# Four products for the decay sums of the delta rule, and one weight split moved ahead of a tile's split at the start of the FFN

## The chip, the core and the metric

The kernel runs on one core of a Trainium2 chip. A core has five engines that run side by side and wait for each other by semaphores: TensorE (PE in the profile; its weight loads stand apart as PEld), VectorE (DVE), ScalarE (ACT), GpSimd (POOL) and SyncE (SP, which here only issues DMAs). Each engine works through its own list of instructions strictly in the order in which they were written into it. The metric is the device time of one execution in microseconds (us), and of several executions the median.

## The reference, cut to what matters

One decoder layer is computed for a prompt (512 tokens with 16 learned tokens ahead of them) and for 8 samples of 8 tokens. Two places of it matter here. In the delta rule the log decays `g` of each token and head are summed up inside their chunk:

```
gcum = jnp.cumsum(gc, axis=-1)
...
g_last = g_i[..., -1:]
s = (s * jnp.exp(g_last)[..., None]
     + jnp.einsum('bhcd,bhce->bhde', k_i * jnp.exp(g_last - g_i)[..., None], v_new))
```

so both the running sum and the sum over the whole chunk are needed. In the FFN the normalised input is multiplied by a matrix of 1024 rows and 2 x 2816 columns:

```
xn = rmsnorm(x, p['ln_ffn_pre'])
up, gate = jnp.split(xn @ p['w_ffn_in'], 2, axis=-1)
gate, new_ffn_conv = causal_dwconv(gate, ffn_conv_buf, p['ffn_conv_w'], p['ffn_conv_b'])
x = x + rmsnorm((jax.nn.gelu(gate) * up) @ p['w_down'], p['ln_ffn_post'])
```

## The kernel before

**Split products.** Large products are made of three fast ones: each operand is split into a rounded high part and the rest. `split` (lines 312 to 314) does that with a CAST on ScalarE (line 313) and a subtraction on VectorE (line 314); a product then takes high by high, low by high and high by low. All matmuls stand under line 271 of `mm`, all transposes under line 419, so the profile tells them apart by the names of their tiles.

**Decay sums.** `gdn_decays` (from line 588) has the tokens in five chunks: four of 128 tokens and a tail of 80 (`NTL`). For each chunk it multiplies a constant matrix (an upper triangle for the running sum, ones for the whole sum; others for the tail, which holds the samples and the learned tokens) by the chunk's `g` of 4 heads: 10 plain fp32 products of 4 columns each, into one PSUM tile that VectorE copies to `gc` (lines 605 and 606). TensorE meets them at 71.5 us, among the projections and the attention over the cache.

**Start of the FFN.** The end of `out_proj` interleaves the output projection's last products with the first products of the FFN. The normalised rows come in five tiles of tokens (`TILES`); `turn(i, end)` transposes one tile on TensorE into two PSUM tiles, and `put_f` splits these into the blocks that the FFN multiplies by: `fhi`/`flo` with a tag of two figures, the first for the upper or lower half of the 1024 rows, the second for the half of the tokens. The fifth tile (`turn(4, ...)`) goes into `fhi12`/`flo12` and `fhi22`/`flo22`, the second half of the tokens. `turn` also returns `sums`, three VectorE operations that start the sums for the later steps.

**First steps.** The FFN's 22 blocks of 128 columns are run one after the other. The first three (`PLAIN`) are done plainly, by `plain_g` (gate) and `plain_u` (up), each for two halves of the tokens; the rest by a seven-product scheme with sums of weights (`sw`, split into `hw`/`lw`) and of inputs (`gf`, `fhit`, `flot`). `ffn_in` takes over from `out_proj` with the first half of step 0 done, then issues the first half of step 1 (`plain_g(sts[1], 0)`, whose weights were split in `out_proj`, and `plain_u(sts[1], 0)`, whose weights `plain_w(0, 1)` loads as two `wraw` tiles and splits into `hw`/`lw`), then the second halves of step 0 and step 1, then step 2.

**What sets the order.** The program is written as Python calls in one order; a scheduler then lays out each engine's list with a model of its own, moving instructions where data allow. Pools hold a fixed number of buffers per tag (3 `wraw`, 2 `whi`, 6 `hw`), so a load waits until the tile three loads back has been split. SP issues the loads of weights in order, each wait holding up all that come after.

Of the kernel before, what the change touches and what calls it, by code (L numbers as in the profile page):

```python
# [33 lines left out]
NS = NB * TS  # L34
# [8 lines left out]
CHUNKS = tuple((128 * c, 128) for c in range(4)) + ((CS, NS + NM),)  # L43
TAIL = 4
NTL = NS + NM
# [105 lines left out]
class Body:  # L151
# [437 lines left out]
    def gdn_decays(self):  # L589

        nc = self.nc
        nch = len(CHUNKS)

        def kept(tag):
            return self.t(self.keep, [128, nch, H], tag)

        p = self.ps("t")[:, : 8 * nch].rearrange("p (c e) -> p c e", e=8)
        for i, (c0, n) in enumerate(CHUNKS):
            up = self.c("upper_t", n) if i == TAIL else self.c("upper")
            tot = self.c("same_t", n) if i == TAIL else self.c("ones")  # L600
            self.mm(p[:n, i, 0:4], up, self.g[:n, i, :], start=True, stop=True)
            self.mm(p[:n, i, 4:8], tot, self.g[:n, i, :], start=True, stop=True)
        self.gc = self.t(self.keep, [128, nch, 8], "gc")
        nc.vector.memset(self.gc, 0.0)
        nc.vector.tensor_copy(self.gc[:, 0:4], p[:, 0:4])
        nc.vector.tensor_copy(self.gc[:NTL, 4], p[:NTL, 4])
        self.neg_eg = kept("neg_eg")
        nc.scalar.activation(self.neg_eg, self.gc[:, :, 0:4], AF.Exp)
        nc.vector.tensor_scalar(self.neg_eg, self.neg_eg, -1.0, None, op0=ALU.mult)
        self.ek = kept("ek")  # L610
        nc.vector.tensor_tensor(out=self.ek, in0=self.gc[:, :, 4:8], in1=self.gc[:, :, 0:4], op=ALU.subtract)
        nc.scalar.activation(self.ek, self.ek, AF.Exp)
# [971 lines left out]
    def out_proj(self, pool, wo0, swo, sm):  # L1584
# [9 lines left out]
        ys, sums, ends = {}, {}, {}  # L1594
# [41 lines left out]
        def turn(i, end):  # L1636
            n, xs, ps = self.TILES[i][1], ys.pop(i), []
            with self.tc.issue_after(end):
                for g in range(2):
                    p = self.ps4("t")  # L1640
                    for k in range(4):
                        ch = 4 * g + k
                        self.transpose(p[:, k, :n], xs[:n, 128 * ch : 128 * ch + 128])
                    ps.append(p)
            c = 128 * ((i - 1) % 2) + 34
            c = slice(c, c + 128)
            for g, p in enumerate(ps):
                if i:
                    self.put_f(g, i > 2, c, p)
                else:  # L1650
                    self.put_f(g, 0, slice(32, 34), p[:, :, NS : NS + 2])
                    for half in range(2):
                        self.put_f(g, half, slice(0, 32), p[:, :, 32 * half : 32 * half + 32])

            def sums():
                r1, r2 = (r[:, :, c] for r in self.r12)
                h11, l11 = (e.bitcast(F32)[:, :, c] for e in f["11"])
                nc.vector.tensor_tensor(out=r1, in0=ps[0], in1=h11, op=ALU.subtract)
                nc.vector.tensor_tensor(out=r1, in0=r1, in1=l11, op=ALU.subtract)
                nc.vector.tensor_tensor(out=r2, in0=ps[1], in1=r1, op=ALU.subtract)  # L1660

            return sums

        def first(c0):
            w, ps = self.weight(a["w_ffn_in"][0], c0), self.psd()[:, :NC]
# [3 lines left out]
        n = self.TILES[0][1]  # L1669
# [8 lines left out]
        product(2, 1)  # L1678
        finish(2)
        turn(0, ends[2, 1])  # L1680
        product(3, 0)
        turn(1, ends[3, 0])
        product(4, 0)
        swo.close()
        self.ftpool = self.pool(sm, "ft", side="right")
        turn_consts = self.ffn_consts()
        self.r12 = [self.t(self.ftpool, [128, 4, NC], tag) for tag in ("fhit4", "flot4")]
        turn(2, ends[4, 0])
        product(3, 1)
        finish(3)  # L1690
# [5 lines left out]
        w1 = [self.t(self.ftpool, [128, 8, 128], tag, F32R) for tag in ("fhit3", "flot3")]  # L1696
# [94 lines left out]
    def ffn_in(self, firsts, sf, gx):  # L1791
# [76 lines left out]
        def begin(st):  # L1868
            st["pre"] = self.t(pool, [128, 514 + 80], "fpre", bufs=2)
# [85 lines left out]
        def plain_w(c0, m):  # L1955
            if m == 1 and c0:
                return w1
            if m != 1:
                return self.weight(w, c0 + 128 * m)
            his, los = [], []  # L1960
            for raw in self.raw_w(w, c0 + 128 * m):
                hi, lo = (self.t(w7, [128, 4, 128], tag, F32R, bufs=n) for tag, n in (("hw", 6), ("lw", 6)))
                self.split(hi, lo, raw)
                his += [hi[:, k] for k in range(4)]
                los += [lo[:, k] for k in range(4)]
            return his, los
# [16 lines left out]

        def plain_u(st, half):
            if not half:
                st["wu"] = plain_w(0, st["m"])
            ps = self.psd()[:, :NC]
            end = self.plain(ps, st["wu"], half)
            st["u", half] = ps
            return end  # L1990
# [4 lines left out]

        sts, waiting = [{"m": m} for m in range(PLAIN)], []
        st = sts[0]
        (st["wg"], ps, _), (st["wu"], u, _), w1, more = firsts
        begin(st)
        copy_g(st, 0, ps)  # L2000
        st["u", 0] = u
        plain_g(sts[1], 0)
        end = plain_u(sts[1], 0)
        more()
        sums = self.sums(gx)
        next(sums)
        with self.tc.issue_after(end):
            plain_g(st, 1)
            conv(st)
            plain_u(st, 1)  # L2010
        plain_end(st)
        next(sums)
        st = sts[1]
        with self.tc.issue_after(end):
            plain_g(st, 1)
            conv(st)
            plain_u(st, 1)
# [16 lines left out]
        for m in range(PLAIN, NF):  # L2034
            st = nxt
# [194 lines left out]
```

## Time and profile before

| | |
|---|---|
| time, median of 3 executions | 1150.32 us |
| the three | 1149.95, 1150.32, 1154.78 us |
| time of the profiled execution | 1154.05 us |
| its span in the profile | 1152.3 us |
| mean granted TensorE clock in it | 0.993 |
| PE busy | 1123.5 us, 98% |
| DVE busy | 715.7 us, 62% |
| ACT busy | 539.0 us, 47% |
| POOL busy | 220.6 us, 19% |
| DMA, mean | 136 GB/s |

The profile is of one execution: all times in it count from the span's start. A row of the timeline has the start, the duration, the engine, the line, the operation, its tiles (out<-in), their shape, and in brackets the idle time of the engine ahead of it with what ended it. Matmuls overlap, so the distance from start to start, not the duration, is what one costs in a row of many. "PEclk" is the TensorE clock that the throttle granted, as a share of full speed.

### The profile page before, as it was taken

Reading aid. Unit: us, or ns where it says so; the run is one execution under the profiler, and the core shown is the slowest. Engines: PE = TensorE matmul, PEld = TensorE weight load, DVE = VectorE, ACT = ScalarE, POOL = GpSimd, SP = SyncE. Lnnn points to the kernel's source line nnn. Section 1 sums busy time; section 2 is a strip of 40 time slices with the busy share of each in tenths; the row PEclk is TensorE's granted clock in tenths of the full one; section 3 lists DMA queues with packets and bytes.
Section 4 is the critical chain, followed back from the end, with each engine's and each line's share of the span. In section 5 each row is a group of like instructions: output and inputs, shape, how many; then the busy total and the mean of one; then the engine's idle time right before and its main releaser. Section 6 shows DMA issues by size and latency. Waiting matters only on the chain.

```text
span 1152.3 us, 23630 instructions
## 1 busy us (share of the span) xinstructions
PE 1123.5 (98%) x8689; PEld 1009.0 (88%) x8689; DVE 715.7 (62%) x1874; ACT 539.0 (47%) x1308; POOL 220.6 (19%) x344
## 2 busy tenths in 40 slices
PE   8999999999999999999999999999999999999997
PEld 7987887787787787789999977899999999999996
DVE  5456666695485386484343764499889898832323
ACT  5234545464465365442432444365555655732321
POOL 3122221120120010010000003323445444200000
PEclk9999999999999999999999999999999999999998
DMA  6366336737746856822232454223333332432322
GB/s 190 81 222 191 107 98 200 250 109 261 246 145 220 292 176 209 262 64 74 56 94 65 128 175 147 91 73 102 102 87 100 93 94 73 144 96 75 102 75 82
DMA packets 184205, 157.04 MB, mean 136 GB/s; under 512 B 12555, under 2 KB 146258, under 8 KB 184089
## 3 DMA queue, kind: packets, MB, share of 16 engines
q1 hardware_dynamic: 179569, 147.01, 42.0%
q0 software_dynamic: 3264, 5.16, 1.5%
q10 hardware_dynamic: 1256, 3.35, 1.0%
q8 instruction: 69, 1.13, 0.4%
q14 instruction: 47, 0.39, 0.1%
HBM read 145.60 MB, written 9.88 MB: 135 GB/s over the span
## 4 chain that ended last, share of the span: by engine, by line
PE 77%; issue 13%; ACT 3%; DVE 3%; POOL 3%; DMA 1%; DVEq 0%; POOLq 0%; ACTq 0%; SPq 0%
PE ps_d L271 28%; PE ps_t L271 18%; PE ps_g L271 15%; PE ps_s L271 7%; PE ps_t L419 7%; ACT KT L1420 1%; PE ps_m L271 1%; POOL grr L383 1%; POOL gf L383 0%; DVE cy L671 0%; DMA page<-in_cache_v 0%; POOL hss L383 0%; PE lnb L271 0%; ACT whi L313 0%; ACT st L877 0%
## 5 line engine op out<-in xcount | busy, mean ns | idle before, releaser
L271 PE MATMUL ps_d<-xhi,whi 128*128 128x256 f32 (+2 forms) x704 | 218.7, 311 | 0.4 <-ACT xhi L313 0.4
L314 DVE TENSOR_TENSOR wlo<-wraw,whi 128x512 fp32r<-128x512 f32 (+1 forms) x194 | 135.8, 716 | 126.0 <-ACT whi L313 125.3
L271 PE MATMUL ps_d<-xhi,wlo 128*128 128x256 f32 (+2 forms) x704 | 214.1, 304 | 0.0
L271 PE MATMUL ps_d<-xlo,whi 128*128 128x256 f32 (+2 forms) x704 | 213.9, 304 | 0.1
L313 ACT CAST whi<-wraw 128x512 fp32r<-128x512 f32 (+1 forms) x198 | 117.4, 612 | 180.0 <-PE ps_d L271 97.0
L271 PEld LDWEIGHTS ps_d<-xhi,whi 128*128 128x128 f32 x704 | 134.5, 191 | 6.1 <-issue 3.8
L271 PEld LDWEIGHTS ps_d<-xlo,whi 128*128 128x128 f32 x704 | 134.8, 192 | 3.1 <-issue 2.4
L271 PEld LDWEIGHTS ps_d<-xhi,wlo 128*128 128x128 f32 x704 | 134.7, 191 | 1.6 <-issue 1.0
L1420 ACT COPY KT<-ps_t 128x512 f32<-128x512 f32 x106 | 57.2, 603 | 31.3 <-PE ps_t L419 30.8
L419 PE MATMUL ps_t<-consts,page 128*128 128x128 f32 x512 | 67.8, 279 | 0.3
L271 PE MATMUL ps_t<-fhit,hw 128*128 128x290 f32 x228 | 68.0, 298 | 0.0
L271 PE MATMUL ps_t<-flot,hw 128*128 128x290 f32 x228 | 67.7, 297 | 0.0
L271 PE MATMUL ps_t<-fhit,lw 128*128 128x290 f32 x228 | 67.6, 297 | 0.0
L419 PEld LDWEIGHTS ps_t<-consts,page 128*128 128x128 f32 x512 | 55.6, 140 | 13.7 <-issue 6.7
L313 ACT CAST hw<-sw 128x512 fp32r<-128x512 f32 x76 | 47.2, 622 | 41.3 <-PE ps_g L271 19.9
L314 DVE TENSOR_TENSOR lw<-sw,hw 128x512 fp32r<-128x512 f32 x76 | 59.7, 786 | 6.6 <-ACT hw L313 6.5
L271 PEld LDWEIGHTS ps_t<-flot,hw 128*128 128x128 f32 x228 | 43.3, 190 | 0.0
L271 PEld LDWEIGHTS ps_t<-fhit,lw 128*128 128x128 f32 x228 | 43.1, 189 | 0.0
L271 PEld LDWEIGHTS ps_t<-fhit,hw 128*128 128x128 f32 x228 | 43.0, 189 | 0.0
L1908 DVE SCALAR_TENSOR_TENSOR fy<-fpre,fw,fy 128x592 f32<-128x592 f32 x44 | 36.5, 830 | 2.2 <-ACT fy L1906 1.6
L271 PE MATMUL ps_s<-page,pT 128*32 128x256 f32 x512 | 35.1, 385 | 1.4 <-DMA page<-in_cache_v 1.3
L271 PE MATMUL ps_s<-KT,qb 128*32 128x256 f32 x512 | 35.7, 385 | 0.6
(693 smaller groups left out, 3000.6 us busy)
## 6 DMA issues: line engine op xcount, KB each, us to landing
page<-in_cache_k SPq DMA_DIRECT2D x128, 256.0 KB, 4.4
page<-in_cache_v SPq DMA_DIRECT2D x128, 256.0 KB, 4.2
wraw<-in_w_in SPq DMA_DIRECT2D x88, 256.0 KB, 3.1
wraw<-in_w_ffn_in SPq DMA_DIRECT2D x50, 256.0 KB, 3.1
wraw<-in_w_down SPq DMA_DIRECT2D x40, 256.0 KB, 3.2
raw<-in_w_ffn_in SPq DMA_DIRECT2D x38, 256.0 KB, 2.9
wraw<-in_w_out SPq DMA_DIRECT2D x16, 256.0 KB, 2.9
x<-in_x_prompt SPq DMA_DIRECT2D x4, 512.0 KB, 6.8
```

The lines of the kernel that those rows point to most:

```text
L271: return self.nc.tensor.matmul(out, lhsT, rhs, **kw).ins
L313: self.nc.scalar.copy(hi, raw)
L314: (eng or self.nc.vector).tensor_tensor(out=lo, in0=raw, in1=hi.bitcast(F32), op=ALU.subtract)
L383: nc.gpsimd.tensor_tensor(out=dst, in0=dst, in1=self.mhalf[:rows, :n], op=ALU.pow)
L419: self.nc.tensor.transpose(out, in_, self.ident[:k, :k])
L1420: copy(kt[:, :, 128 * j : 128 * j + 128], tp)
L1908: nc.vector.scalar_tensor_tensor(out=y, in0=pre[:, j : j + 592], scalar=fw[:, m, 16 + j : 17 + j], in1=y, op0=ALU.mult, op1=ALU.add)
```

## The change

Two edits. The decay sums are made in 4 products in place of 10: the four whole chunks lie beside each other in `g`, so one product of 4 x 4 columns takes all of them for the running sum and one for the whole sum, and the tail has its own two of 4 columns. And the up weights of step 1 are loaded and split by a call that stands ahead of the split of the fifth turned tile: `turn` no longer calls `put_f` for that tile itself but hands out `put`, which `ffn_in` calls after `plain_w(0, 1)`.

```
-        for i, (c0, n) in enumerate(CHUNKS):
-            up = self.c("upper_t", n) if i == TAIL else self.c("upper")
-            tot = self.c("same_t", n) if i == TAIL else self.c("ones")
-            self.mm(p[:n, i, 0:4], up, self.g[:n, i, :], start=True, stop=True)
-            self.mm(p[:n, i, 4:8], tot, self.g[:n, i, :], start=True, stop=True)
+        for e, (whole, tail) in enumerate((("upper", "upper_t"), ("ones", "same_t"))):
+            sl = slice(4 * e, 4 * e + 4)
+            self.mm(p[:, 0:4, sl], self.c(whole), self.g[:, 0:4, :], start=True, stop=True)
+            self.mm(p[:NTL, 4, sl], self.c(tail, NTL), self.g[:NTL, 4, :], start=True, stop=True)
...
-            for g, p in enumerate(ps):
-                if i:
-                    self.put_f(g, i > 2, c, p)
...
+            def put():
+                for g, p in enumerate(ps):
+                    if i:
+                        self.put_f(g, i > 2, c, p)
...
+            if i < 4:
+                put()
...
-            return sums
+            return sums if i < 4 else (put, sums)
...
         def plain_u(st, half):
             if not half:
-                st["wu"] = plain_w(0, st["m"])
+                st["wu"] = st.get("wu") or plain_w(0, st["m"])
...
-        (st["wg"], ps, _), (st["wu"], u, _), w1, more = firsts
+        (st["wg"], ps, _), (st["wu"], u, _), w1, (put, more) = firsts
+        sts[1]["wu"] = plain_w(0, 1)
+        put()
         begin(st)
```

On TensorE the rest of the list stays as it was; only the decay sums differ. Before, at the place of the decay sums (`xhi`, `xlo`, `whi` belong to a projection around them, `kvt` to new keys and values):

```order
L419 MATMUL ps_t_938<-consts_66,kvt_848 80x128
L271 MATMUL ps_d_980<-xhi_6_84,whi_972 128x256
L271 MATMUL ps_t_947<-g_661,consts_66 128x4 x8
L271 MATMUL ps_t_947<-g_661,consts_66 80x4 x2
L271 MATMUL ps_d_980<-xlo_7_85,whi_972 128x256
```

and now:

```order
L271 MATMUL ps_d_974<-xhi_6_84,whi_966 128x256
L271 MATMUL ps_t_947<-g_661,consts_66 128x4x4
L271 MATMUL ps_t_947<-g_661,consts_66 80x4
L271 MATMUL ps_t_947<-g_661,consts_66 128x4x4
L271 MATMUL ps_t_947<-g_661,consts_66 80x4
L271 MATMUL ps_d_974<-xlo_7_85,whi_966 128x256
```

Eight products of whole chunks became two, and the two of the tail stayed; their neighbours are the same.

ScalarE's list at the start of the FFN, before (`fhi12`, `fhi22` are the fifth tile, `fpre` the copied gate products of steps 0 and 1, `hw` the up weights of step 1):

```order
L313 CAST fhi12_1736_9258<-ps_t_1832_9880 128x4x128
L313 CAST fhi22_1740_9262<-ps_t_1833_9885 128x4x128
L1971 COPY fpre_1852_9922<-ps_d_1818_9768 128x258
L1972 COPY fpre_1852_9922<-ps_d_1818_9768 128x4x8
L1971 COPY fpre_1853_9925<-ps_g_1854_9926 128x258
L1972 COPY fpre_1853_9925<-ps_g_1854_9926 128x4x8
L313 CAST hw_1857_9957<-wraw_1855_9953 128x512
L313 CAST hw_1859_9961<-wraw_1856_9955 128x512
```

and now:

```order
L313 CAST fhi12_1736_9252<-ps_t_1832_9874 128x4x128
L313 CAST hw_1854_9916<-wraw_1852_9912 128x512
L313 CAST hw_1856_9920<-wraw_1853_9914 128x512
L313 CAST fhi22_1740_9256<-ps_t_1833_9879 128x4x128
L1975 COPY fpre_1858_9928<-ps_d_1818_9762 128x258
L1976 COPY fpre_1858_9928<-ps_d_1818_9762 128x4x8
L1975 COPY fpre_1859_9931<-ps_g_1860_9932 128x258
L1976 COPY fpre_1859_9931<-ps_g_1860_9932 128x4x8
```

The two weight casts moved past the second cast of the fifth tile and the four copies, but still stand behind the first cast of that tile. VectorE's list at the same place, before:

```order
L1660 TENSOR_TENSOR flot4_1798_9650<-ps_t_1820_9798,fhit4_1797_9649 128x4x128
L314 TENSOR_TENSOR flo12_1737_9259<-ps_t_1832_9880,fhi12_1736_9258 128x4x128
L314 TENSOR_TENSOR flo22_1741_9263<-ps_t_1833_9885,fhi22_1740_9262 128x4x128
L1658 TENSOR_TENSOR fhit4_1797_9649<-ps_t_1832_9880,fhi11_1734_9256 128x4x128
L314 TENSOR_TENSOR lw_1858_9958<-wraw_1855_9953,hw_1857_9957 128x512
L314 TENSOR_TENSOR lw_1860_9962<-wraw_1856_9955,hw_1859_9961 128x512
```

and now:

```order
L1664 TENSOR_TENSOR flot4_1798_9644<-ps_t_1820_9792,fhit4_1797_9643 128x4x128
L314 TENSOR_TENSOR flo12_1737_9253<-ps_t_1832_9874,fhi12_1736_9252 128x4x128
L314 TENSOR_TENSOR lw_1855_9917<-wraw_1852_9912,hw_1854_9916 128x512
L314 TENSOR_TENSOR lw_1857_9921<-wraw_1853_9914,hw_1856_9920 128x512
L314 TENSOR_TENSOR flo22_1741_9257<-ps_t_1833_9879,fhi22_1740_9256 128x4x128
L1662 TENSOR_TENSOR fhit4_1797_9643<-ps_t_1832_9874,fhi11_1734_9250 128x4x128
```

The two subtractions of the weights moved past two operations. Further down, some two dozen rows on VectorE and a dozen on ScalarE stand a few places earlier or later up to the middle of the first step of the seven-product scheme, and on SP two loads for that scheme (`raw`) now stand behind two loads of `wraw`; from there on all lists are as before.

More of the change, by code (lines that the diff above doesn't have):

```diff
@@ L1646, in turn @@
             c = slice(c, c + 128)
-            for g, p in enumerate(ps):
-                if i:
-                    self.put_f(g, i > 2, c, p)
[L1650 to L1653, printed above, removed]
+            def put():
+                for g, p in enumerate(ps):
+                    if i:
+                        self.put_f(g, i > 2, c, p)
+                    else:
+                        self.put_f(g, 0, slice(32, 34), p[:, :, NS : NS + 2])
+                        for half in range(2):
+                            self.put_f(g, half, slice(0, 32), p[:, :, 32 * half : 32 * half + 32])
+            if i < 4:
+                put()
             def sums():
```

## The prediction

> **What bounds the kernel now.** I read the page first, then the waits of TensorE by stretch, then the timeline at the two places of the change, then the granted clock in stretches of 3.41 us.
>
> ```profile
> PE 1123.5 (98%) x8689; PEld 1009.0 (88%) x8689; DVE 715.7 (62%) x1874; ACT 539.0 (47%) x1308; POOL 220.6 (19%) x344
> PE 77%; issue 13%; ACT 3%; DVE 3%; POOL 3%; DMA 1%; DVEq 0%; POOLq 0%; ACTq 0%; SPq 0%
> ```
>
> TensorE is busy 98% of the span and carries 77% of the chain that ended last. So a microsecond taken out of its list, or out of one of its waits, should reach the end unless a later wait swallows it. The waits of TensorE between the two places (74 to 748 us) and behind the second (754 to the end) are few:
>
> ```profile
> PE ps_s L271 <- DMA page<-in_cache_v: 1.3, 2, 0.9
> ...
> PE ps_t L419 <- ACT yT L2126: 0.8, 1, 0.8
> ```
>
> (us in total, times, longest; the first row is of 15 between the places, none over 2.0 us in total, the last is the longer of two behind.) Only the 1.3 us are on a DMA, and the loads of those pages are themselves let go by TensorE:
>
> ```profile
> SPq L1399 <- PE ps_t L419: 59.3, 35, 11.3
> SPq L1399 <- PE ps_s L271: 58.0, 28, 9.3
> ```
>
> So an earlier TensorE brings earlier loads, and I let all of an early gain through; the bound below is that none of it comes through.
>
> The clock is the less visible part. These are stretches of 3.41 us (PE busy with its instructions in brackets, then the granted clock):
>
> ```profile
> 71.03:74.44 3.41, 3.40 (x32) 1.00 1.04 364
> 74.44:77.85 3.41, 3.41 (x19) 0.50 1.05 383
> 712.73:716.15 3.42, 1.58 (x10) 1.00 0.38 153
> 716.15:719.56 3.41, 3.41 (x10) 0.50 0.46 159
> 746.87:750.28 3.41, 1.49 (x13) 1.00 0.83 236
> 750.28:753.69 3.41, 3.41 (x13) 0.50 0.45 130
> ```
>
> Three times behind the start the clock is halved for just one such stretch. The starts lie 641.71 and 34.13 us apart, 188 and 10 times 3.413: the stretches sit on a fixed grid, and each halved one follows one in which TensorE did little. In two of these it was idle about half the time; in the first it was "busy", but with 20 passes of four columns. Both places of the change stand there.
>
> **The change part by part: the decay sums.**
>
> ```profile
> 70.68 0.71 PE L419 MATMUL ps_t<-consts,kvt 128*128 128x128 f32 x5
> 71.52 2.23 PE L271 MATMUL ps_t<-g,consts 128*128 128x4 f32 x20
> 73.61 0.36 PE L271 MATMUL ps_d<-xlo,whi 128*128 128x256 f32 x1
> 72.65 1.10 PE L271 MATMUL ps_t<-g,consts 128*128 128x4 f32 x10
> ```
>
> Each fp32 product is two passes: 20 for 10 products, from 71.52 to 73.61, 2.09 us. The last row is of a view that starts later: the last ten passes (six of a whole chunk, four of the tail) take 73.61 - 72.65 = 0.96, so the ten whole ones ahead take 1.13, or 0.113 each. Twelve whole passes go: **1.36 us**. The four whole passes that stay have 16 columns, not 4. If they cost as much as passes of 128 columns, which run at (70.68 - 68.75) / 16 = 0.121 in this row,
>
> ```profile
> 68.75 2.10 PE L419 MATMUL ps_t<-consts,page 128*128 128x128 f32 x16
> ```
>
> 0.03 comes off; below, if nothing reaches the end, 0. I take 1.36, as TensorE is neither waiting just ahead of the next matmul nor just behind. `gc` is ready earlier and no one waits for it there.
>
> **The wait at the start of the FFN.** First columns are start and duration:
>
> ```profile
> 747.59 1.30 ACT L313 CAST fhi<-ps_t 128x512 fp32r<-128x512 f32 x2 [1.39 <-PE ps_t L419]
> 749.47 1.18 ACT L313 CAST hw<-wraw 128x512 fp32r<-128x512 f32 x2
> 748.21 1.40 DVE L314 TENSOR_TENSOR flo<-ps_t,fhi 128x512 fp32r<-128x512 f32 x2 [0.26 <-ACT fhi L313]
> 750.16 1.29 DVE L314 TENSOR_TENSOR lw<-wraw,hw 128x512 fp32r<-128x512 f32 x2
> 747.67 0.60 PE L419 MATMUL ps_t<-consts,y 128*128 128x128 f32 x4
> 750.18 0.55 PE L271 MATMUL ps_s<-fhi,hw 128*128 128x290 f32 x1 [1.92 <-ACT hw L313]
> 750.91 0.61 PE L271 MATMUL ps_s<-fhi,lw 128*128 128x290 f32 x1
> 732.46 1.04 SPq L309 DMA_DIRECT2D wraw<-in_w_ffn_in  x2
> ```
>
> TensorE waits 1.92 us for the first cast of the weights, and its third matmul for the first `lw`. The weights were asked for at 732.46 and so are long there; the casts only stood behind six others. In the new list the first weight cast still stands behind `fhi12`, which waits for the transposes: it starts one cast after 747.59, at 747.59 + 0.60 = 748.2 and ends near 748.8, so the first matmul starts at about 748.9. On VectorE `flo12` runs from 748.21 for 0.7 and the first `lw` from about 748.85 to 749.5: the third matmul starts at 749.57, not 750.91. Gain **1.34 us**. Between zero and 1.92 (no wait left) lie the bounds; since everything from the third matmul on hangs on that `lw`, I keep 1.34.
>
> What is late in its place: `fhi22`/`flo22` end 1.3 us later, near 750.85. They are first read in the second half of the next product, which starts at
>
> ```profile
> 755.19 0.30 PE L271 MATMUL ps_t<-fhi,whi 128*128 128x290 f32 x1
> 768.37 0.30 PE L271 MATMUL ps_g<-fhi,wlo 128*128 128x290 f32 x1
> 765.18 1.89 DVE L314 TENSOR_TENSOR wlo<-wraw,whi 128x512 fp32r<-128x512 f32 x3
> 773.72 1.75 POOL L1826 TENSOR_TENSOR sw<-raw,raw 128x512 f32<-128x512 f32 x1 [1.23 <-DVE lw L314]
> ```
>
> at 755.19 + 12 x 0.134 = 756.8, after the change 754.0 at the earliest: 3.1 us of cover. The four `fpre` copies move back 1 us and free PSUM that is wanted at 761.6. Two `raw` loads now stand behind a `wraw` load that waits for the new `lw`, some 4 us later than now; their first reader is GpSimd at 773.72. All these cost nothing while that cover lasts, and a microsecond of TensorE for each beyond it.
>
> **The clock.** What a halved stretch costs comes from the distances of starts, first at the decay sums, then at the FFN:
>
> ```profile
> 74.05 0.28 PE L271 MATMUL ps_d<-xlo,whi 128*128 128x256 f32 x1
> 74.17 0.28 PE L271 MATMUL ps_d<-xhi,wlo 128*128 128x256 f32 x1
> 74.79 0.41 PE L271 MATMUL ps_d<-xhi,whi 128*128 128x256 f32 x1
> 75.00 0.41 PE L271 MATMUL ps_d<-xlo,whi 128*128 128x256 f32 x1
> ...
> 752.05 0.44 PE L271 MATMUL ps_s<-fhi,hw 128*128 128x290 f32 x1
> 752.29 0.44 PE L271 MATMUL ps_s<-flo,hw 128*128 128x290 f32 x1
> 753.86 0.29 PE L271 MATMUL ps_s<-fhi,lw 128*128 128x290 f32 x1
> 753.99 0.30 PE L271 MATMUL ps_s<-fhi,hw 128*128 128x290 f32 x1
> ```
>
> 0.12 becomes 0.21, 0.13 becomes 0.24: of 3.41 us some 45% is lost, **1.53 us** each. After the change the low work of the decay sums lasts 0.73 us, not 2.09, and the FFN's wait is split into about 0.6 and 0.4 with matmuls between: neither leaves a stretch as empty as the 1.49 or 1.58 of 3.41 above, so I expect neither to halve the clock. The stretch behind 712.73 is not touched. Bounds for this term in one execution: 0 and 3.06.
>
> [...]
>
> **The sum.** Against the profiled execution: 1154.05 - 1.36 - 1.34 - 3.06 = 1148.3, and 1151.35 if the clock term is nothing. The median is another matter. It lies 3.73 us under the profiled execution, 2.4 times the price of a halved stretch; the grid starts anew against each execution, so I read the spread of the three times (1149.95 to 1154.78) as none to three such stretches. An execution like the median then had about 0.6 of them (3 - 2.4), two thirds of it at the two places: 0.4 x 1.53 = 0.6. So 1150.32 - 2.70 - 0.6 = 1147.0; I say **1147.1**.
>
> **The rivals.** A: *the wait moves on*. TensorE comes up to 2.9 us earlier to `ps_g` of step 2, whose third matmul (768.37) needs a `wlo` that ends near 765.9 now, 2.5 us ahead. In the new list that `wlo` stands behind the same operations as before, in another order, and VectorE has no gap in the 4 us ahead of it, so it can hardly come earlier. By the row lengths I get it some 0.9 to 1.3 us ahead of its matmul; if it is wrong by that much more, the wait gain goes: 1150.32 - 1.36 = 1149.0. [...] C: *the median holds all of both places' cost*: 1150.32 - 2.70 - 3.06 = 1144.6; against it stands the spread, in which the fastest lies only 0.4 below the median. D: *slower*. VectorE works strictly in order, and the convolution of step 0 (`fy`, line 1908) moved ahead of an operation that waits for nothing. `fy` waits for ScalarE, which waits for TensorE:
>
> ```profile
> 760.80 0.83 DVE L1908 SCALAR_TENSOR_TENSOR fy<-fpre,fw,fy 128x592 f32<-128x592 f32 x1 [1.36 <-ACT fy L1906]
> ```
>
> now 1.36 us idle. If that idle time grows, everything behind it, the `wlo` too, slips. It decides from the point at which `wlo` ends beyond 767.0 (768.37 - 1.34), and is slower than before once TensorE waits over 2.7 us, or 1.2 with a halved stretch behind it (1.53). Three microseconds of slip would give 1147.1 + 3 + 1.53 = 1151.6. Against it: `fy`'s input comes earlier too, by the same 1.34.
>
> **How the numbers follow.** Forecast 0.62 (1145.5 to 1148.9), A 0.12, B 0.09, C 0.13, D 0.04. The range goes from just above C's 1144.6 to A with one more halved stretch on a bad grid, 1149.0 + 1.5: 1144.9 to 1150.3. A measurement of this kernel tells about 0.5% (5.75 us) from no change, so faster begins at 1144.57 and slower at 1156.07. Half and more of C and a little of the forecast's edge lie beyond the first: 0.13. Of D only a slip of some 8 us would pass the second: 0.03. The rest, 0.84, is within 0.5%: a gain of 2 to 4 us that this bound does not tell from none.
>
> **What would show it.** Right: eight passes for `g` in about 0.75 us; the first `ps_s` matmul of step 1 some 0.6 us behind the transposes, no halved stretch behind either place, no wait of TensorE at `ps_g` of step 2. Wrong: a new TensorE wait on `wlo` or `flo`, the pitch of the four new passes far over 0.12, a halved clock behind one of the two places, or a median that moves by under 1 us.

## The result and the profile after

| | before | changed |
|---|---|---|
| median of the first comparison, 10 executions each | 1153.88 us | 1147.30 us (1145.09 to 1151.86) |
| median of a later one, 34 and 12 executions | 1152.31 us | 1148.25 us |
| span of the profiled execution | 1152.3 us | 1145.7 us |

The changed kernel takes 0.9957 of the time before (95% interval 0.994 to 0.9975), and 0.9973 (0.9958 to 0.9988) the second time: 3 to 7 us less by the first, 1 to 5 by the second. One execution of the later comparison on each side, 1348.90 us before and 3498.77 us changed, lies far from all others and is left out of its ratio. The rows of the changed kernel's page that answer to the first two of the prediction:

```profile
PE 1118.0 (98%) x8677; PEld 1003.2 (88%) x8677; DVE 727.3 (63%) x1874; ACT 532.2 (46%) x1308; POOL 229.0 (20%) x344
PE 76%; issue 12%; DVE 5%; ACT 3%; POOL 3%; DMA 1%; DVEq 0%; POOLq 0%; ACTq 0%; SPq 0%
```

Twelve TensorE instructions are gone, and the bound is the same. One row goes the wrong way: VectorE is 11.6 us longer busy with as many instructions; its `wlo` subtractions alone last 763 ns in the mean, not 716. This comes with the weight split (727.4 us and 757 ns with the split alone, 715.1 us and 715 ns with the sums alone), and no wait of TensorE shows for it. One place where an operation of VectorE lasts longer than elsewhere (`lw`, 1.62 us where it took 0.68) matters below.

The timeline of TensorE at the decay sums (start, duration):

```profile
70.30 0.90 PE L271 MATMUL ps_t<-g,consts 128*128 128x16 f32 x8
71.06 0.37 PE L271 MATMUL ps_d<-xlo,whi 128*128 128x256 f32 x1
```

From the first pass to the next product 0.76 us, where it was 2.09. At the start of the FFN, TensorE, ScalarE, VectorE and GpSimd:

```profile
743.49 0.60 PE L419 MATMUL ps_t<-consts,y 128*128 128x128 f32 x4
744.58 0.40 PE L271 MATMUL ps_s<-fhi,hw 128*128 128x290 f32 x1 [0.49 <-ACT hw L313]
745.39 0.40 PE L271 MATMUL ps_s<-fhi,lw 128*128 128x290 f32 x1 [0.28 <-DVE lw L314]
...
743.42 0.59 ACT L313 CAST fhi<-ps_t 128x512 fp32r<-128x512 f32 x1 [1.40 <-PE ps_t L419]
743.90 1.14 ACT L313 CAST hw<-wraw 128x512 fp32r<-128x512 f32 x2
...
744.65 2.38 DVE L314 TENSOR_TENSOR lw<-wraw,hw 128x512 fp32r<-128x512 f32 x2
...
744.87 1.60 POOL L1830 TENSOR_TENSOR sw<-raw,raw 128x512 f32<-128x512 f32 x1 [1.21 <-DMA raw<-in_w_ffn_in]
```

The weight casts begin 0.41 us behind the start of the transposes, and the third matmul starts 745.39 - 743.49 = 1.90 us after the transposes do, against 750.91 - 747.67 = 3.24 before. The two `lw` took 1.29 together before; they take 2.38. The waits of TensorE from 746 us to the end are these two, as before:

```profile
PE ps_t L419 <- ACT yT L2132: 0.8, 1, 0.8
PE ps_t L419 <- DVE yT L2129: 0.4, 1, 0.4
```

So nothing took the place of the wait. Stretches of 3.41 us of the changed kernel, on its grid (PE busy, then the granted clock):

```profile
69.83:73.24 3.41, 3.40 (x31) 1.00 1.02 324
73.24:76.65 3.41, 3.41 (x33) 1.00 1.05 389
708.12:711.53 3.41, 1.56 (x11) 1.00 0.38 154
711.53:714.95 3.42, 3.42 (x9) 0.50 0.49 158
742.25:745.67 3.42, 2.65 (x20) 1.00 0.47 139
745.67:749.08 3.41, 3.41 (x26) 1.00 0.46 134
```

Behind both places of the change the clock is whole. The one halved stretch between the start and 1125 us is at the place that the change does not touch. The distances between the rows shown add up to the difference of the spans:

| from | to | before | changed | less |
|---|---|---|---|---|
| start | first pass of the sums | 71.52 | 70.30 | 1.22 |
| there | next product | 2.09 | 0.76 | 1.33 |
| there | the fifth tile's last four transposes | 674.06 | 672.43 | 1.63 |
| there | third `ps_s` matmul | 3.24 | 1.90 | 1.34 |
| there | end of the span | 401.39 | 400.31 | 1.08 |

The first row has nothing to do with the change: it goes with the moment after the start at which the clock is first granted in full, 16.4 us in one execution, 11.8 in the other. The third and the last each hold a halved stretch that is gone. What the one behind the sums cost shows in how far the first `ps_m` matmul behind it lies from that next product, before and then changed:

```profile
78.02 0.94 PE L271 MATMUL ps_m<-kT,qT 64*128 64x400 f32 x4
```

```profile
73.95 0.94 PE L271 MATMUL ps_m<-kT,qT 64*128 64x400 f32 x4
```

That is 78.02 - 73.61 = 4.41 against 73.95 - 71.06 = 2.89, so 1.52 us of the 1.63 in the third row.

### The profile page after: what moved, and what is told of

Read it like the earlier page. It is cut to its first block, busy times and chain, and to the rows that moved or that the text cites. A ratio compares the mean times of both kernels' runs of the same rounds, so it can differ in the third digit from the quotient of the medians.

```text
span 1145.7 us, 23610 instructions
## 1 busy us (share of the span) xinstructions
PE 1118.0 (98%) x8677; PEld 1003.2 (88%) x8677; DVE 727.3 (63%) x1874; ACT 532.2 (46%) x1308; POOL 229.0 (20%) x344
## 4 chain that ended last, share of the span: by engine, by line
PE 76%; issue 12%; DVE 5%; ACT 3%; POOL 3%; DMA 1%; DVEq 0%; POOLq 0%; ACTq 0%; SPq 0%
PE ps_d L271 28%; PE ps_t L271 18%; PE ps_g L271 15%; PE ps_s L271 7%; PE ps_t L419 7%; ACT KT L1419 1%; PE ps_m L271 1%; DVE cy L670 1%; POOL grr L383 1%; POOL gf L383 0%; DMA page<-in_cache_v 0%; DVE row L990 0%; DVE row L991 0%; DVE xc L992 0%; POOL hss L383 0%
## 5 line engine op out<-in xcount | busy, mean ns | idle before, releaser
L314 DVE TENSOR_TENSOR wlo<-wraw,whi 128x512 fp32r<-128x512 f32 (+1 forms) x194 | 145.2, 763 | 125.2 <-ACT whi L313 124.5
L314 DVE TENSOR_TENSOR lw<-sw,hw 128x512 fp32r<-128x512 f32 x76 | 67.9, 893 | 6.0 <-ACT hw L313 6.0
L1910 ACT ACTIVATE fy<-fpre,fw 128x592 f32<-128x592 f32 x22 | 19.4, 884 | 42.0 <-DVE fpre L1870 41.9
```

What stands on the lines that cost most here:

```text
L314: (eng or self.nc.vector).tensor_tensor(out=lo, in0=raw, in1=hi.bitcast(F32), op=ALU.subtract)
L1910: nc.scalar.activation(y, pre[:, 0:592], AF.Identity, bias=fw[:, m, 19:20], scale=fw[:, m, 16:17])
```

## The experiments

Each was compared with the kernel before on the same chip, 6 to 12 executions against 25 to 35; in the order of the runs. The ratio is the one of the comparison itself and can differ from that of the two medians by some 0.1%.

| kernel | median us | kernel before | ratio, 95% interval |
|---|---|---|---|
| sums alone | 1150.14 | 1152.62 | 0.9979 (0.9968 to 0.999) |
| split alone | 1151.83 | 1152.62 | 1.0001 (0.9987 to 1.0014) |
| ten products of 40 columns | 1150.25 | 1152.62 | 0.9984 (0.9972 to 0.9996) |
| wait filled | 1151.29 | 1152.62 | 0.9988 (0.9977 to 0.9999) |
| changed kernel again | 1148.25 | 1152.31 | 0.9973 (0.9958 to 0.9988) |
| constants into the wait | 1148.89 | 1152.31 | 0.998 (0.9968 to 0.9992) |
| split alone, sum on VectorE | 1150.63 | 1152.31 | 0.9994 (0.9979 to 1.001) |
| changed, sum on VectorE | 1147.01 | 1152.31 | 0.9966 (0.9952 to 0.998) |
| sums doubled | 1156.43 | 1152.12 | 1.0041 (1.0025 to 1.0057) |
| turn ahead of finish | 1143.78 | 1152.12 | 0.9933 (0.9913 to 0.9953) |
| changed, sum on VectorE, again | 1147.93 | 1152.12 | 0.9965 (0.9951 to 0.9979) |
| split alone, again | 1152.49 | 1152.12 | 1.0002 (0.9988 to 1.0016) |

**Each half of the change by itself.** The sums alone: only the first hunk of the diff.

> The kernel before with the decay sums in 4 products, nothing else. My theory (two direct gains, plus a halved clock that each of the two places causes in a part of the executions): 1.36 us less in every execution, and 1.53 less in those in which the place halved the clock, taken as half to all of them: 2.1 to 2.9 us under the kernel before. No halved stretch behind the sums in the profile. Rival 'all of it is the FFN': 0 to 0.5 us. Rival 'the clock has another cause': 1.36 us, and still a halved stretch near 75 us in some executions.

The split alone: only the hunks behind it.

> The kernel before with the weight split moved ahead, the decay sums in 10 products. My theory: 1.34 us less in every execution and 1.53 in those in which the wait halved the clock: 2.0 to 2.9 us under the kernel before; with the sums alone it adds up to the whole change. TensorE waits about 0.5 us for hw and 0.3 for lw. Rival 'all of it is the sums': 0 to 0.5 us. Rival 'the clock has another cause': 1.34 us.

The sums alone gained 1.2 to 3.7 us, as expected. The split alone gained nothing, a miss. Its timeline at the place shows why (TensorE, VectorE, GpSimd), and below it stands the view of the tile `lw` there (durations in ns: least, median, most):

```profile
747.03 0.60 PE L419 MATMUL ps_t<-consts,y 128*128 128x128 f32 x4
749.86 0.40 PE L271 MATMUL ps_s<-fhi,lw 128*128 128x290 f32 x1 [1.22 <-DVE lw L314]
...
748.19 2.22 DVE L314 TENSOR_TENSOR lw<-wraw,hw 128x512 fp32r<-128x512 f32 x2
...
747.98 1.27 POOL L1831 TENSOR_TENSOR sw<-raw,raw 128x512 f32<-128x512 f32 x1 [0.78 <-DMA raw<-in_w_ffn_in]
```

```profile
L314 DVE TENSOR_TENSOR lw<-wraw,hw x2: 678/1148/1619, 748.2 to 749.7; 128x512 fp32r<-128x512 f32 x2
```

The casts did move, but the first `lw` took 1.62 us, not 0.68. GpSimd had begun the first sum of weights for the seven-product scheme 0.21 us ahead of it, and `lw` ended 0.56 us after that sum did (747.98 + 1.27 = 749.25; 748.19 + 1.62 = 749.81). So the third matmul came 2.83 us behind the transposes, a gain of 0.41 where 1.34 was expected. In the changed kernel the sum began 0.22 us *behind* the first `lw`, and it was the second one that was held, for which TensorE does not wait.

**Is it GpSimd?** The same split, with that one sum moved to VectorE, behind both `lw`; and the same in the changed kernel:

```diff
-        def weights_s(st):
+        def weights_s(st, eng=nc.gpsimd):
...
-            combine(st, "s1", a21, a22, ALU.add)
+            combine(st, "s1", a21, a22, ALU.add, eng)
...
-        weights_s(nxt)
+        weights_s(nxt, nc.vector)
```

> The split of wu alone (as in the run of the split by itself, which gained nothing), but the first sw<-raw,raw of the Strassen steps is done by VectorE behind both lw, not by GpSimd. Theory (GpSimd's subtraction on the same memory doubled the first lw from 0.68 to 1.62 us and so took the gain away): both lw at 0.68 to 0.72 us, the third ps_s matmul 1.9 us behind the transposes, 0.9 to 1.0 us under the split alone, so 1.1 to 1.6 us under the kernel before, as far as VectorE's one more operation of about 0.7 us hides. Rival (lw was late or long for another cause: the loads of raw into SBUF, a wait for its buffers): lw 1.6 us again and the third matmul 2.8 us behind, no gain over the split alone. The ten 4-column products stand as before: a halved stretch behind the sums in this profile by the theory of the clock.

> The changed kernel, with the first sw<-raw,raw on VectorE behind both lw. Theory: both lw at 0.68 to 0.72 us (second one 1.78 in the changed kernel's profile), third ps_s matmul 1.9 us behind the transposes in each execution and not in some of them only: 0 to 0.9 us under the changed kernel, by how often the collision with the first lw falls there. Rival (the extra operation on VectorE makes gf, flot or wlo late): 0.2 to 1.0 us over the changed kernel, with a TensorE wait at step 2 or at the first Strassen step. No halved stretch behind the sums, one at the FFN place in at most one execution of three.

With the split alone and the sum on VectorE, the tile `lw` and the third matmul:

```profile
L314 DVE TENSOR_TENSOR lw<-wraw,hw x2: 682/683/684, 744.2 to 744.8; 128x512 fp32r<-128x512 f32 x2
```

```profile
743.00 0.60 PE L419 MATMUL ps_t<-consts,y 128*128 128x128 f32 x4
744.90 0.40 PE L271 MATMUL ps_s<-fhi,lw 128*128 128x290 f32 x1 [0.28 <-DVE lw L314]
```

Both `lw` at 0.68 and 1.90 us from transposes to third matmul: without GpSimd's sum beside it, the first no longer takes 1.62. In the time the step is 0.8 us (0.9994 against 1.0001), under what the intervals resolve; the trace carries this verdict, not the time. The changed kernel with the sum on VectorE could not be told from the changed kernel, in either of its runs; in both profiles of the latter the collision fell on the second `lw` anyway.

> The changed kernel once more, beside the next three on one chip. Theory: eight passes for the sums in 0.75 us, no halved stretch right behind them (none in three profiles without ten 4-column products, one in each of three with them); third ps_s matmul 1.9 to 2.9 us behind the transposes, by where GpSimd's first sw<-raw,raw falls: 1.9 where it begins after the first lw has, up to 2.9 where it begins before. Time 2.5 to 6.5 us under the kernel before. Rival (the clock's stretches fall by chance and have nothing to do with the sums): a halved stretch behind the sums in about half of the profiles of either kind, so also here or in the two runs beside it with four products.

> The changed kernel with the first sw<-raw,raw on VectorE once more, to compare the run above with on one chip. 4.0 to 5.5 us under the kernel before (1147.01 against 1152.31 at first); both lw at 0.64 us, third ps_s matmul 1.89 us behind the transposes; no halved stretch behind the sums; one at 708 to 715 in about two executions of five.

> The split of wu alone once more. If the collision of GpSimd's sw<-raw,raw with the first lw is a matter of when the raw loads land against the work, it may fall on the first lw (third ps_s matmul 2.83 us behind the transposes, as at first) or on the second (1.89 us, as in both profiles of the changed kernel); if 1.62 us belongs to this kernel's order of work, 2.83 again. Time 0 to 1.3 us under the kernel before, where the first run had 0.0 (0.13% up to 0.14% either way).

The split alone, again, GpSimd and the third matmul:

```profile
748.65 1.27 POOL L1831 TENSOR_TENSOR sw<-raw,raw 128x512 f32<-128x512 f32 x1 [0.73 <-DMA raw<-in_w_ffn_in]
...
750.52 0.40 PE L271 MATMUL ps_s<-fhi,lw 128*128 128x290 f32 x1 [1.17 <-DVE lw L314]
```

748.65 + 1.27 = 749.92, and the matmul 0.60 later: the same collision, and again no gain in the time. The changed kernel, again, had 1.9 us, eight passes in 0.75, and no halved stretch between its start and 1125 us. So in four profiles of four the side of the collision went with the kernel, by a margin of 0.1 to 0.25 us between a DMA's landing and VectorE's place in its list. Why the loads land on that side in each is not settled.

**The clock.** Three runs asked whether the four-column passes and the wait were what halved it. First the ten products with 40 columns each, every number ten times over: as many passes, as much TensorE time, more work in it.

```diff
-            self.mm(p[:n, i, 0:4], up, self.g[:n, i, :], start=True, stop=True)
-            self.mm(p[:n, i, 4:8], tot, self.g[:n, i, :], start=True, stop=True)
+            self.mm(pw[:n, i, 0:40], up, self.g[:n, i, :].unsqueeze(1).to_broadcast([n, 10, 4]), start=True, stop=True)
+            self.mm(pw[:n, i, 40:80], tot, self.g[:n, i, :].unsqueeze(1).to_broadcast([n, 10, 4]), start=True, stop=True)
...
```

> The kernel before, its 10 products for the decay sums kept, but each with 40 columns in place of 4: the 4 columns of g are read ten times over, and 4 of the 40 results are used. The 20 passes should keep their 0.113 us, so the direct cost stays; only the array has more to do meanwhile. My theory (the clock is halved where few columns move, not where TensorE lists no instruction): no direct gain, but no halved stretch behind the sums: 0.8 to 1.5 us under the kernel before in the median, none at 75 us in the profile. [...]

Then the wait at the FFN filled with twelve matmuls whose product is written over:

```diff
...
+            if st["m"] == 1 and not half:
+                with self.tc.issue_after(self.last_turned):
+                  for k in range(12):
+                    self.mm(ps, w1[0][k % 4], f["11"][0][:, k % 4], start=True, stop=True)
             end = self.plain(ps, st["wu"], half)
```

> The kernel before, with 12 extra matmuls of 290 columns, with operands that are there, put into the 1.92 us wait for the weights at the start of the FFN; they write the PSUM tile that the real products then overwrite, 12 x 0.134 = 1.6 us. All other lists are those of before. My theory: the third real matmul still starts 3.2 us behind the last transposes, so no direct gain, but no halved stretch behind the wait: 0.7 to 1.5 us under the kernel before in the median. Rival 'the clock has another cause': the same as before or up to 0.3 us slower, with a halved stretch still there.

Timeline of the ten wide products, and stretches on that run's grid; then TensorE in the filled wait:

```profile
70.34 2.27 PE L271 MATMUL ps_t<-g,consts 128*128 128x40 f32 x20
72.44 0.37 PE L271 MATMUL ps_d<-xlo,whi 128*128 128x256 f32 x1
```

```profile
69.23:72.64 3.41, 3.40 (x31) 1.00 1.04 365
72.64:76.06 3.42, 3.42 (x27) 1.00 1.05 392
```

```profile
746.31 0.60 PE L419 MATMUL ps_t<-consts,y 128*128 128x128 f32 x4
746.66 1.86 PE L271 MATMUL ps_s<-fhi,fhit 128*128 128x290 f32 x12
...
749.55 0.40 PE L271 MATMUL ps_s<-fhi,lw 128*128 128x290 f32 x1 [0.19 <-DVE lw L314]
```

The wide sums take the same 2.10 us and their stretch the same 3.40 us "busy", yet the next stretch is whole, and the kernel is 0.5 to 3.2 us faster with nothing shortened. The filled wait is as long as before (3.24) and the kernel still 0.1 to 2.7 us faster. No list of work got shorter in either, so I take both for gains of the clock; that of the filled wait lies only just outside the noise.

But the split with the sum on VectorE had the ten narrow products and no halved stretch behind them, against what was expected of it. Its grid may tell why:

```profile
68.49:71.91 3.42, 3.41 (x37) 1.00 1.03 348
71.91:75.32 3.41, 3.41 (x33) 1.00 1.05 380
75.32:78.73 3.41, 3.41 (x33) 1.00 1.06 376
```

The sums ran from 71.65 to 73.75 there, so a bound fell into them, and no stretch held all 20 passes. That gave a sharper theory, tested by issuing each of the ten products twice:

```diff
-            self.mm(p[:n, i, 0:4], up, self.g[:n, i, :], start=True, stop=True)
-            self.mm(p[:n, i, 4:8], tot, self.g[:n, i, :], start=True, stop=True)
+            for _ in range(2):
+                self.mm(p[:n, i, 0:4], up, self.g[:n, i, :], start=True, stop=True)
+                self.mm(p[:n, i, 4:8], tot, self.g[:n, i, :], start=True, stop=True)
```

> The kernel before, with each of the ten 4-column products of the sums issued twice (the second writes the same numbers again): 40 narrow passes on TensorE, 4.2 us. Theory (the clock is set by windows of 3.41 us that run on from the start of the execution; a window in which these passes take 2.1 us or more of TensorE's time is followed by a halved one; with 2.09 us in all that depends on where the window's bounds fall, so it came in three profiles of four and not in the split run with VectorE's subtraction, whose bound fell 0.26 us into the sums): with 4.2 us every position of the bounds leaves a window with at least 2.1 us, so there is a halved stretch right behind or in the sums in this profile and in each execution: 2.1 + 0.5 to 1.5, so 2.6 to 3.6 us over the kernel before. Rival (halved stretches fall there by chance or by another engine's load): 2.1 us over it, and a halved stretch in this profile in half of the cases.

Timeline, and stretches of TensorE on its grid:

```profile
70.92 5.69 PE L271 MATMUL ps_t<-g,consts 128*128 128x4 f32 x40
76.46 0.56 PE L271 MATMUL ps_d<-xlo,whi 128*128 128x256 f32 x1
```

```profile
70.13:73.55 3.42, 3.41 (x31) 1.00 1.04 339
73.55:76.96 3.41, 3.41 (x20) 0.50 1.06 391
76.96:80.38 3.42, 3.42 (x18) 0.50 0.50 148
80.38:83.79 3.41, 3.41 (x33) 1.00 0.00 0
```

Here TensorE is "busy" to the last digit and its clock is halved for two stretches running. The size was put too low: 2.9 to 6.6 us over the kernel before by the interval, 2.6 to 3.6 expected. Twice 2.09 is 4.18; they last 5.54, as those in the halved stretch run slower too: at the 0.105 us each of the single passes (2.09 / 20), 25 are through at 73.55, and the other 15 take 2.91 us, 0.19 each by this estimate. That stretch, narrow passes for most of its length, is followed by a second halved one.

Over the 14 profiles of this study the columns that TensorE moved can be counted in each stretch of the grid between 22 and 1125 us, each matmul shared out over its duration. The middle stretch has some 7,300. Of 4,527 stretches 17 were followed by a halved one: all 11 with fewer than 1,915 columns, 4 of the 8 with 1,921 to 2,297, and 2 of the 4,508 above (2,549 and 2,796). These figures move by some hundred columns with how a matmul on a bound is counted, so they show an order, not a threshold; whether the clock is set by columns, or by something that goes with them, is not shown.

By place: behind the sums 5 of 6 profiles with narrow passes as many as before or more, none of 8 with the four products or with 40 columns. Behind the FFN's wait 2 of 4 that keep it, none of 10 that fill or shorten it. At the third place, the second tile's transposes, 6 of the 13 that leave it alone. There is a fourth, at 188 to 196 us, which no kernel here changes: 3 of 14, those in which TensorE had waited 2.2 to 2.4 us in one piece for a `page` load (1.0 to 2.6 us over two waits in the others). The doubled sums' second stretch makes up the 17.

**What was left of the wait.** The changed kernel still idles about 0.8 us there. The transposes of the convolution's constants were moved into it:

```diff
-        with self.tc.issue_after(u0[2]):
-            turn_consts()
...
-        plain_g(sts[1], 0)
+        end = plain_g(sts[1], 0)
+        with self.tc.issue_after(end):
+            turn_consts()
```

> The changed kernel, with the 26 small transposes of the FFN convolution's constants (1.46 us of TensorE's time at 738.3 to 739.7) put into what is left of the wait behind the fifth tile's transposes. Theory (TensorE stands idle there for about 1.1 us of 1.90, for the hw casts and the lw subtractions, and those begin when the fifth tile's transposes are through, not by the clock): the transposes and all that hangs on them come 1.46 us sooner, the constants run in the wait, and the kernel is 0.8 to 1.2 us under the changed kernel. Rival (what ends the wait is a load or another engine's work that does not come sooner): within 0.3 us of it. A halved stretch at this place, if there was one, is gone in either case, or as rare as before.

```profile
741.21 1.09 PE L419 MATMUL ps_t<-consts,y 128*128 128x128 f32 x8 [0.57 <-DVE y L403]
742.59 0.71 PE L419 MATMUL ps_t<-consts,fhit 20*128 20x20 f32 x9 [0.28 <-PE ps_t L419]
```

No gain: the rival's case. With 1.46 us of cover gone from ahead of the fifth tile's transposes, these now wait themselves, 0.57 us, for VectorE's `y`. The idle time moved upstream.

**A version that beats both.** The third place is the largest idle time of TensorE left near the change: in the kernel before, with the same rows shifted in the changed one,

```profile
712.44 0.60 PE L419 MATMUL ps_t<-consts,y 128*128 128x128 f32 x4
714.18 0.63 PE L419 MATMUL ps_t<-consts,y 128*128 128x128 f32 x4 [1.15 <-DVE flo L314]
715.50 0.47 PE L271 MATMUL ps_t<-owhi,gt 128*128 128x512 f32 x1 [0.69 <-DVE flo L314]
```

The PSUM tiles are free only when the first tile's splits are done, and those stood behind the third tile's finishing. Written the other way round, on top of the changed kernel with the sum on VectorE:

```diff
-        finish(2)
         turn(0, ends[2, 1])
+        finish(2)
```

> The changed kernel with the first sw<-raw,raw on VectorE, and the turn of the first tile of the output projection written ahead of the finishing of the third, so that the four hi casts of the turn are ahead of ojunk<-xr on ScalarE, and the four lo subtractions ahead of r and y<-xr on VectorE. TensorE waited twice there for these subtractions (1.15 and 0.70 us at 708 to 711.4 in the changed kernel's profile, ahead of the second half of the second tile's transposes and of ps_t<-owhi), and the low share of work in that window is what the halved stretch at 711.5 followed. Theory: both waits shrink by 1.2 to 1.85 us together, no halved stretch behind them; 1.2 to 2.5 us under the run beside it with the subtraction alone, 4.5 to 7 us under the kernel before. Rival (the third tile's y comes late for its own transposes, as the fifth's did when the constants were moved behind it): a TensorE wait for y at the third tile's transposes of 0.5 us or more, and a gain under 0.7.

TensorE at the place, a stretch with it, and the waits of TensorE from 704 to 760 us:

```profile
707.66 1.03 PE L419 MATMUL ps_t<-consts,y 128*128 128x128 f32 x8
708.45 0.48 PE L271 MATMUL ps_t<-owhi,gt 128*128 128x512 f32 x1
```

```profile
706.02:709.44 3.42, 3.42 (x20) 1.00 0.40 159
709.44:712.85 3.41, 3.41 (x16) 1.00 0.33 97
```

```profile
PE ps_s L271 <- ACT hw L313: 0.5, 1, 0.5
PE ps_s L271 <- DVE lw L314: 0.3, 1, 0.3
```

Both waits are gone: 0.79 us from the transposes to the next product, 3.06 before. No wait for `y` appeared, so the rival falls. It takes 1143.78 us, 0.9933 of the kernel before and 3.7 us (about 2 to 5, from the means of the two) less than the run beside it without this edit, more than the 1.2 to 2.5 expected: the place gave 2.27, not 1.85, and 6 of the 13 profiles without this edit have a halved stretch behind it.

## Why the prediction was right, and where not

The forecast of 1147.1 us stands beside 1147.30 and 1148.25 us. Part of that closeness is luck: it started from the median of three, 1150.32, and the kernel before has 1152.1 to 1153.9 in longer series. As a step, 3.2 us (0.28%) were forecast and 0.43% and 0.27% measured; both intervals hold it.

- **The sums, 1.36**: 1.33 in the trace. The passes' pitch hardly changed with 16 columns: eight passes took 0.76, where four whole ones at 0.113 and the tail's four at the 0.07 of before (0.96 less six at 0.113) make 0.73.
- **The wait, 1.34**: 1.34 in the changed kernel's profile, with casts and first matmul close to where they were put. But the step "everything from the third matmul on hangs on that `lw`" took `lw` at the length it had where nothing ran beside it. GpSimd's sum stood in the trace of before at the very place,

```profile
748.62 1.27 POOL L1826 TENSOR_TENSOR sw<-raw,raw 128x512 f32<-128x512 f32 x1 [0.77 <-DMA raw<-in_w_ffn_in]
```

  beside the second of VectorE's two `flo`, which reads one operand from PSUM and took 0.69 us, as the first did. The prediction looked at GpSimd only at 773.72. Moving `lw` forward moved it under this sum. The bounds of 0 to 1.92 hold both outcomes, but the rivals did not name it.
- **Cover for what became late**: `fhi22`, `fpre` and the `raw` loads cost nothing; no TensorE wait shows behind the place. Rivals A and D fall with that.
- **The clock, 0.6**: right in kind, too small. The price of 1.53 for a halved stretch holds behind the sums (1.52); behind the FFN's wait it was 1.1 (last row of the table). The step that failed is the count: the low median was read as an execution with 0.6 halved stretches, 0.4 of them at the two places, and three times were too few for that. With 4 of 5 profiles behind the ten narrow products and 2 of 4 behind the wait, the two places had 1.3 halved stretches an execution before, or 4/5 x 1.52 + 1/2 x 1.1 = 1.8 us, and none now. That is an estimate from a handful of profiles; it lies about midway between the forecast's 0.6 and the 3.06 of rival C. With 1.8 the sum is 1.33 + 1.34 + 1.8 = 4.5 us, between the two measured steps (0.43% and 0.27% are 5.0 and 3.1).
- **Rival B** (0.09) is that the halved clock has another cause than the two places. It falls by the wide sums (the next stretch at 1.00) and the doubled sums (two stretches at 0.50), and the filled wait agrees.

## What to carry to other kernels

Ask of TensorE not only whether it is busy but how many columns it moves: here ten products of four columns (2.09 us) were followed by 3.41 us at half the clock in 4 of 5 profiles, and a wait at the FFN that was 1.92 us in the kernel before in 2 of 4, and that spread is worth taking out. Before an operation on VectorE is moved forward, look at what GpSimd does at the place where it lands, and at where the inputs lie: here `lw`, with both in SBUF, took 1.62 us beside a sum of GpSimd, not 0.68, and `flo`, with one in PSUM, its usual 0.69. When a wait is filled with work taken from ahead of it, ask which wait that work was hiding.

## What was unexpected of the hardware

- In these runs the halved stretches went with how few columns the stretch ahead had moved, and came also where TensorE had hardly stood idle: 40 passes of four columns, in a stretch with TensorE busy for 3.41 of 3.42 us, were followed by two halved ones. In the kernel before, idle times of 1.15 and 0.69 us (712.44 to 715.50) were followed by one.
- Wherever a VectorE operation with both inputs in SBUF and a GpSimd sum of weights with both inputs in SBUF ran at once, up to 830 us in the profiles of the kernel before and the changed one, at least one of the two took longer than alone. In the two runs of the split alone the first `lw`, begun 0.21 and 0.25 us behind GpSimd's sum, ended 0.56 and 0.55 us behind the end of that sum, about its own length alone from start to start (0.61, two in 1.29 with 0.68 each). In the changed kernel the second `lw`, 1.78 us long, also ended 0.56 behind it (745.25 + 1.78 = 747.03; 744.87 + 1.60 = 746.47). It can be the other way round: in the same profile a sum of GpSimd that began at 766.81 us, 0.16 behind such a VectorE operation, took 4.83 us, not 1.27, while that one and five more, all of 0.68 to 0.75 us, followed each other without a gap until the next began at 770.41. What makes the one or the other longer is not shown.
- The first pass of the sums starts at 70.2 to 70.7 us where the clock is first granted in full by 12 us, and at 70.9 to 72.2 where that comes at 15.5 to 17.5 (14 profiles): about 1.2 us, and up to 2, of a comparison of single executions goes with the place of the grid, not with the kernel.
